# A fourth slot for weighted context tokens, with the gate tiles moved into shared slots, in a hybrid SSD and RG-LRU block

## The chip, the core and the metric

The kernel runs on one core of a Trainium2 chip. The metric is the device time of one launch in microseconds (us), the median of several runs. The engines are named as in the profile: PE (TensorE, with PEld for its weight loads), DVE (VectorE), ACT (ScalarE) and SP (SyncE, which here issues the transfers).

## What is computed

One layer of a diffusion backbone over 256 latent tokens with a prefix of 256 context tokens, width 2048. A projection is split among two mixers, a state-space one (SSD) and a gated linear recurrence (RG-LRU), which are merged by gates; a feed-forward block follows. The recurrences of the latent tokens start from the final states of the context tokens.

```python
# D_MODEL 2048, SEQ 256, CTX_LEN 256, 32 SSD heads of 64 in 4 groups, state 128, chunk 128; all float32
mod   = silu(c) @ w_ada + b_ada                       # shifts, scales, gates; mod_c from c_ctx
hc, h = modulate(rmsnorm(ctx)), modulate(rmsnorm(x))  # 256 context and 256 latent tokens
z, xs, bs, cs, dt, xr, yr = split(h @ w_in)           # the same weights for hc
# (A) SSD mixer, both directions, from the context's final states
xs, bs, cs = silu(dwconv(xs, bs, cs));  dt = softplus(dt + bias)
states = einsum('bcqgn,bcqge,bcqgep->bcgepn', B, decay_to_end, xdt)
y = einsum(C B, L, xdt) + einsum(C, exp(a_cum), entering) + d_skip * xs
o_s = rmsnorm(y * silu(z)) @ w_out_ssd
# (B) RG-LRU mixer, both directions, column-major
r, i = sigmoid(xr_heads @ w_a + b_a), sigmoid(xr_heads @ w_x + b_x)
a = exp(-8 * r * softplus(-lam));  u = sqrt(1 - a*a) * (i * xr)
o_r = (linear_scan(a, u) * gelu(yr)) @ w_out_lru
g_s, g_r = sigmoid(h @ w_gate + b_gate)
x = x + g_m * ((g_s * o_s + g_r * o_r) @ w_o)
x = x + g_f * swiglu(modulate(rmsnorm(x)), w13, w2);  out = rmsnorm(x)
```

## The kernel before

**Products.** Nearly all time goes into products of activations with weights, 440 MB of weights in float32 that are each read once. Every float32 value is split into two halves of a shorter format, high and low; a product is three matmuls, high by high, high by low and low by high (L184 to L186 for 512 tokens, L188 to L190 for 256). The activations stand split in T1 and T2. The weights come in pieces of 512 KB: SP loads `raw` (L156), ACT casts the high half `wh` (L172), DVE subtracts for the low half `wl` (L173). Each of these tiles has a ring of 4 slots (RING). A job of 16 row blocks has two pieces and 48 matmuls into one bank of PSUM; there are three such banks, tag "mm". Then the job's own evacuation reads the bank, and behind each job `run` (L224) puts a piece of other work from the lists `bg` and `turns`.

**LRU stage.** The first jobs are a narrow one for dt, pairs of gate jobs, and xr jobs between them. A gate job computes 128 columns of the mixer's gates; `gate_evac` (L439) copies the bank into a tile gt and sends it to memory, from where it is read much later. After each second xr job an LRU batch is queued: `operands` (casts lh and xh, L477 and L479), `gates` (lg matmuls, L490 to L492, and sigmoids), `decays` (exponentials A and hyperbolic tangents R), `scans`, and the sum of both directions in a tile ro (L519), which goes to memory (L523). All activation functions of ACT are kept in program order by an explicit dependency. The order of the instructions on all engines, PE among them, is set at build time by a list scheduler: it takes what is ready first by its own times, and a tile's slot is given out in the order of the program.

**SSD stage.** From here PE's order is the program's. There are four groups of jobs: four xs jobs, one for B and one for C. Behind the jobs of the next group stand the parts of the group before: `context_tokens` transposes the group's context tokens and writes four weighted copies (`weighted`, L670; DVE, tile xw, 2 KB a partition); `context_states` multiplies them with B, two matmuls for each direction (L708, L709), and writes two more xw; `carried_states` multiplies those (L723); the units follow (operands AC, E, G; products py). In the same stage `ada_rest` (L427 to L432) loads rows of the modulation weights in transfers of 512 KB into the ring of `raw` (rawa) and multiplies and sums them on DVE, two for each job. Then z, yr, the mixers' output projections, w_o and the feed-forward products follow.

**Tags and slots.** A tag is a ring of slots in SBUF. gt has two slots of 1 KB a partition of its own, in the pool `ap`. The tag hv (pool `tp`, 4 slots of 1 KB) is taken by tiles that live briefly: halves (L271), ro (L519), dty (L558) and h2 (L957).

Of the kernel before, what the change touches and what calls it, by code (L numbers as in the profile page):

```python
# [8 lines left out]
F32 = mybir.dt.float32  # L9
# [5 lines left out]
P = 128  # L15
D = 2048
KT = D // P
T = 256
# [36 lines left out]
def hybrid_block(  # L55
# [11 lines left out]
    tp = ctx.enter_context(tc.tile_pool(name="tp", bufs=2))  # L67
# [323 lines left out]
    ap = ap_stack.enter_context(tc.tile_pool(name="ap", bufs=1))  # L391
# [46 lines left out]

    def gate_evac(n):  # L439
        def f(ps):  # L440
            t = ap.tile([P, T], F32, tag="gt", name="gt", bufs=2)
            act.copy(t, ps[:, :T])  # L442
            side.dma_start(gD[n], t)
        return f
# [209 lines left out]
    def ssd_group(g):  # L654
        gp, wt, dec = sd["gp"], sd["wt"], sd["dec"]
# [4 lines left out]
        def heads(t):  # L660
            return t.rearrange("p (h c) -> p h c", h=8)

        def head_scale(t, d):
            return t[:, hs[d]].unsqueeze(2).broadcast_to([P, 8, 64])
# [3 lines left out]
                fn(t, t, AF.Silu)  # L668

        def weighted(ps, blk, d):  # L670
            o = gp.tile([P, 4 * P], F32, tag="xw", name="xw", bufs=3)
            dve.tensor_tensor(heads(o), heads(ps), head_scale(wt[:, blk], d), ALU.mult)
            return o

# [7 lines left out]
        def context_tokens():  # L682

            pb = bank("pB")
            for q in range(4):
                pe.transpose(pb[:, q * P:q * P + P], B[:, q * P:q * P + P], ident)

            pc = bank("pC")
            for c in range(2):
                s = slice(c * P, c * P + P)  # L690
                pe.matmul(pc[:, s], B[:, s], Cm[:, s], start=True, stop=True)
            px = [tokens(2), tokens(3)]
            Bt = st["Bt"] = gp.tile([P, 4, P], F32, tag="Bt", name="Bt")
            act.copy(Bt.rearrange("p a b -> p (a b)"), pb)
            U = st["U"] = gp.tile([P, 2, P], F32, tag="U", name="U")
            L = st["L"] = gp.tile([P, 2, P], F32, tag="L", name="L")
            for i in range(2):
                for d in range(2):
                    st["xc", d, i] = weighted(px[i], 5 + i, d)
            pcv = pc[:, :T].rearrange("p (c i) -> p c i", c=2)  # L700
            dve.tensor_tensor(U, pcv, mU.unsqueeze(1).broadcast_to([P, 2, P]), ALU.mult)
            dve.tensor_tensor(L, pcv, mL.unsqueeze(1).broadcast_to([P, 2, P]), ALU.mult)

        def context_states():
            px = [tokens(0), tokens(1)]
            for d in range(2):
                p0 = bank("p0")
                pe.matmul(p0, st["Bt"][:, 2, :], st["xc", d, 0], start=True, stop=False)  # L708
                pe.matmul(p0, st["Bt"][:, 3, :], st["xc", d, 1], start=False, stop=True)  # L709
                s0 = gp.tile([P, 4 * P], F32, tag="s0", name="s0", bufs=2)  # L710
                act.copy(s0, p0)

                st["S", d, d] = s0
            for q in range(2):
                o = st["xt", q] = gp.tile([P, 4 * P], F32, tag="xt", name="xt", bufs=2)
                act.copy(o, px[q])
                st["xl", q] = weighted(px[q], 4, q)
# [238 lines left out]
    for k in range(KT):  # L956
        t = tp.tile([P, T], F32, tag="hv", name="h2", bufs=4)  # L957
# [95 lines left out]
```

## Time and profile before

| | us |
|---|---|
| median of 3 runs (lowest, highest) | 2048.64 (2040.79, 2052.87) |
| profiled execution | 2049.12 |
| its span | 2047.3 |
| PE busy | 1973.7 (96%) |
| PEld busy | 1685.0 (82%) |
| DVE busy | 1435.0 (70%) |
| ACT busy | 1086.5 (53%) |

The span goes from the first to the last instruction; busy is the time in which the engine has an instruction, and a stretch in which PE is busy need not be one at full clock. The mean granted clock of the span is 0.987 of full speed. The LRU stage lies at about 184 to 505 us, the SSD stage with the gate jobs behind it at 505 to 870 us. The shares are means over stages, so the stages are read apart. Line numbers such as L709 are those of the kernel before.

### The profile page before, as it was taken

Reading aid. Unit: us, or ns where it says so; the run is one execution under the profiler, and the core shown is the slowest. Engines: PE = TensorE matmul, PEld = TensorE weight load, DVE = VectorE, ACT = ScalarE, POOL = GpSimd, SP = SyncE. Lnnn points to the kernel's source line nnn. Section 1 sums busy time; section 2 is a strip of 40 time slices with the busy share of each in tenths; the row PEclk is TensorE's granted clock in tenths of the full one; section 3 lists DMA queues with packets and bytes.
Section 4 is the critical chain, followed back from the end, with each engine's and each line's share of the span. In section 5 each row is a group of like instructions: output and inputs, shape, how many; then the busy total and the mean of one; then the engine's idle time right before and its main releaser. Section 6 shows DMA issues by size and latency. Waiting matters only on the chain.

```text
span 2047.3 us, 30483 instructions
## 1 busy us (share of the span) xinstructions
PE 1973.7 (96%) x11633; PEld 1685.0 (82%) x11633; DVE 1435.0 (70%) x2148; ACT 1086.5 (53%) x1646; POOL 0.2 (0%) x4
## 2 busy tenths in 40 slices
PE   7999999999979898999999999899999999999997
PEld 3678888898757687878888888788888888888887
DVE  5567899985867778778896666766666665555554
ACT  4244889874454454755655544544544444544442
POOL 0000000000000000000000000000000000000000
PEclk9999999999989899999999999999999999999999
DMA  9974444464565568799986655577776765566563
GB/s 374 358 264 153 127 143 154 155 201 146 168 186 169 172 187 261 226 360 324 344 316 212 198 186 194 166 227 233 241 230 229 234 222 186 180 190 189 181 196 125
DMA packets 143266, 440.32 MB, mean 215 GB/s; under 512 B 17424, under 2 KB 36112, under 8 KB 142992
## 3 DMA queue, kind: packets, MB, share of 16 engines
q1 hardware_dynamic: 142752, 437.91, 65.5%
q8 instruction: 91, 1.49, 0.3%
q10 hardware_dynamic: 368, 0.47, 0.1%
q14 instruction: 55, 0.45, 0.1%
HBM read 427.77 MB, written 10.55 MB: 214 GB/s over the span
## 4 chain that ended last, share of the span: by engine, by line
PE 82%; DMA 8%; DVE 4%; ACT 3%; issue 2%; SPq 0%; DVEq 0%; ACTq 0%
PE ps L202 37%; PE ps L203 19%; DMA rawa<-in_dram 6%; PE ps L184 4%; PE ps L185 4%; PE ps L186 3%; PE ps L188 2%; PE ps L189 2%; PE ps L190 2%; DVE wl L173 1%; PE ps L358 1%; PE pa L311 1%; PE ps L359 1%; PE ps L360 1%; DMA raw<-in_dram 1%
## 5 line engine op out<-in xcount | busy, mean ns | idle before, releaser
L202 PE MATMUL ps<-T,wh 128*128 128x512 f32 x3332 | 1174.4, 397 | 6.8 <-DVE T L961 4.5
L173 DVE TENSOR_TENSOR wl<-raw,wh 128x1024 fp32r<-128x1024 f32 (+1 forms) x562 | 677.9, 1207 | 392.6 <-ACT wh L172 390.1
L203 PE MATMUL ps<-T,wl 128*128 128x256 f32 x3332 | 935.9, 281 | 2.4 <-DVE wl L173 2.4
L172 ACT CAST wh<-raw 128x1024 fp32r<-128x1024 f32 (+1 forms) x562 | 581.3, 1037 | 654.9 <-issue 280.9
L202 PEld LDWEIGHTS ps<-T,wh 128*128 128x128 f32 x3332 | 626.9, 188 | 157.9 <-issue 5.3
L203 PEld LDWEIGHTS ps<-T,wl 128*128 128x128 f32 x3332 | 630.7, 189 | 4.2 <-DVE wl L173 3.7
L432 DVE SCALAR_TENSOR_TENSOR rawa<-rawa,sc 128x1024 f32<-128x1024 f32 x128 | 156.3, 1222 | 94.1 <-DMA rawa<-in_dram 93.5
L184 PE MATMUL ps<-T,wh 128*128 128x512 f32 x464 | 187.3, 404 | 0.4 <-ACT gt L442 0.4
L185 PE MATMUL ps<-T,wh 128*128 128x512 f32 x464 | 182.7, 394 | 0.0
L186 PE MATMUL ps<-T,wl 128*128 128x512 f32 x464 | 182.2, 393 | 0.0
L188 PE MATMUL ps<-T,wh 128*128 128x256 f32 x576 | 165.4, 287 | 0.4 <-ACT gt L442 0.4
L189 PE MATMUL ps<-T,wh 128*128 128x256 f32 x576 | 163.4, 284 | 0.0
L190 PE MATMUL ps<-T,wl 128*128 128x256 f32 x576 | 163.4, 284 | 0.0
L188 PEld LDWEIGHTS ps<-T,wh 128*128 128x128 f32 x576 | 110.8, 192 | 3.7 <-issue 1.3
L189 PEld LDWEIGHTS ps<-T,wh 128*128 128x128 f32 x576 | 110.8, 192 | 2.0 <-issue 0.8
L190 PEld LDWEIGHTS ps<-T,wl 128*128 128x128 f32 x576 | 110.7, 192 | 0.9
L184 PEld LDWEIGHTS ps<-T,wh 128*128 128x128 f32 x464 | 88.4, 191 | 22.1 <-issue 2.7
L185 PEld LDWEIGHTS ps<-T,wh 128*128 128x128 f32 x464 | 88.3, 190 | 20.0 <-issue 2.2
L186 PEld LDWEIGHTS ps<-T,wl 128*128 128x128 f32 x464 | 88.1, 190 | 19.1
L106 ACT ACT_TABLE_LOAD x46 | 59.0, 1283 | 0.8
L352 DVE TENSOR_TENSOR wl<-raw,wh 128x896 fp32r<-128x896 f32 x16 | 17.5, 1091 | 45.5 <-ACT wh L351 45.5
L358 PE MATMUL ps<-T,wh 128*128 128x512 f32 x112 | 46.6, 416 | 0.0
(232 smaller groups left out, 1765.8 us busy)
## 6 DMA issues: line engine op xcount, KB each, us to landing
raw<-in_dram SPq DMA_DIRECT2D x546, 512.0 KB, 4.4
rawa<-in_dram SPq DMA_DIRECT2D x128, 512.0 KB, 4.9
wa<-in_dram SPq DMA_DIRECT2D x64, 512.0 KB, 7.5
AC<-acD SPq DMA_DIRECT2D x16, 512.0 KB, 7.0
raw<-in_dram SPq DMA_DIRECT2D x16, 448.0 KB, 7.5
raw<-in_dram SPq DMA_DIRECT2D x18, 256.0 KB, 2.7
X<-in_dram SPq DMA_DIRECT2D x8, 512.0 KB, 7.2
lw<-in_dram SPq DMA_DIRECT2D x16, 256.0 KB, 3.5
```

The lines of the kernel that those rows point to most:

```text
L172: act.copy(h[:, :n], raw[:, :n])
L173: dve.tensor_sub(l[:, :n], raw[:, :n], h[:, :n].bitcast(F32))
L184: pe.matmul(ps, wh, T1[:, k, :], start=s, stop=False)
L185: pe.matmul(ps, wh, T2[:, k, :], start=False, stop=False)
L186: pe.matmul(ps, wl, T1[:, k, :], start=False, stop=e)
L188: pe.matmul(ps[:, :T], wh, T1[:, k, :T], start=s, stop=False)
L189: pe.matmul(ps[:, :T], wh, T2[:, k, :T], start=False, stop=False)
L190: pe.matmul(ps[:, :T], wl, T1[:, k, :T], start=False, stop=e)
L202: pe.matmul(ps, wh, a, start=s, stop=False, skip_group_check=True)
L203: pe.matmul(ps[:, T:], wl, a[:, :T], start=False, stop=e, skip_group_check=True)
L358: pe.matmul(ps0[n], h[:, n, :], T1[:, k, :], start=k == 0, stop=False)
L432: dve.scalar_tensor_tensor(rv, rv, 1.0, sc[:, h * 1024:h * 1024 + 1024], ALU.mult, ALU.mult, accum_out=MP[:, n, h:h + 1])
```

## The change

Two tiles get other slots. xw has four instead of three. gt leaves its own two slots and takes one of the four of the tag hv. The bytes of SBUF in use stay equal: 2 KB a partition are freed and 2 KB are taken.

```diff
--- before.py
+++ after.py
@@ -438,7 +438,7 @@
 
     def gate_evac(n):
         def f(ps):
-            t = ap.tile([P, T], F32, tag="gt", name="gt", bufs=2)
+            t = tp.tile([P, T], F32, tag="hv", name="gt", bufs=4)
             act.copy(t, ps[:, :T])
             side.dma_start(gD[n], t)
         return f
@@ -668,7 +668,7 @@
                 fn(t, t, AF.Silu)
 
         def weighted(ps, blk, d):
-            o = gp.tile([P, 4 * P], F32, tag="xw", name="xw", bufs=3)
+            o = gp.tile([P, 4 * P], F32, tag="xw", name="xw", bufs=4)
             dve.tensor_tensor(heads(o), heads(ps), head_scale(wt[:, blk], d), ALU.mult)
             return o
 
```

The scheduler makes another order of it. On ACT, in the LRU stage, these rows follow each other in the kernel before; the two L442 rows are the copies of the third and the fourth gate, L172 are weight casts, and L106 with lg is a sigmoid of an LRU batch.

```order
L602 COPY wt<-pt 128x320
L172 CAST wh<-raw 128x1024 x2
L442 COPY gt<-ps 128x256
L172 CAST wh<-raw 128x1024 x2
L442 COPY gt<-ps 128x256
L172 CAST wh<-raw 128x1024
L106 ACTIVATE dt_1464<-dt_1464 64x256
L106 ACT_TABLE_LOAD
L106 ACTIVATE R<-lg,V 128x512
L106 ACTIVATE I<-lg,V 128x512
```

In the changed kernel the same place of ACT reads, with neither copy in it:

```order
L602 COPY wt<-pt 128x320
L172 CAST wh<-raw 128x1024 x4
L106 ACTIVATE dt_1464<-dt_1464 64x256
L106 ACT_TABLE_LOAD
L106 ACTIVATE R<-lg,V 128x512
L106 ACTIVATE I<-lg,V 128x512
L602 COPY wt<-pt 128x128
L106 ACTIVATE R<-lg,V 128x512
L477 CAST lh<-lw 128x512
L106 ACTIVATE I<-lg,V 128x512
L479 CAST xh<-xc 128x512
```

On ACT some 50 rows further on, in the exponentials and tangents (A, R) of the second batch, the changed kernel has:

```order
L106 ACT_TABLE_LOAD
L106 ACTIVATE A<-R,SL 128x512
L106 ACTIVATE R<-R,SL 128x512
L106 ACTIVATE A<-R,SL 128x512
L172 CAST wh<-raw 128x1024
L106 ACTIVATE R<-R,SL 128x512
L442 COPY gt<-ps 128x256
L106 ACTIVATE A<-R,SL 128x512
L442 COPY gt<-ps 128x256
L172 CAST wh<-raw 128x1024
L106 ACTIVATE R<-R,SL 128x512
```

The two copies of gt moved from the casts ahead of the first sigmoids to the decays of the second batch.

On PE, the changed kernel has this behind the last matmuls of the fourth gate's product (L188 to L190); pt are transposes of dt, lg the LRU gates' matmuls.

```order
L188 MATMUL ps<-T_94,wh 128x256
L189 MATMUL ps<-T_95,wh 128x256
L190 MATMUL ps<-T_94,wl 128x256
L600 MATMUL pt<-K,dt_1464 128x64 x2
L490 MATMUL lg<-xh,lh 128x512
L491 MATMUL lg<-xl,lh 128x512
L492 MATMUL lg<-xh,ll 128x512
L490 MATMUL lg<-xh,lh 128x512
L491 MATMUL lg<-xl,lh 128x512
L492 MATMUL lg<-xh,ll 128x512
L490 MATMUL lg<-xh,lh 128x512 x4
L491 MATMUL lg<-xl,lh 128x512
```

On PE in the kernel before, the same product is followed by the next product:

```order
L188 MATMUL ps<-T_94,wh 128x256
L189 MATMUL ps<-T_95,wh 128x256
L190 MATMUL ps<-T_94,wl 128x256
L184 MATMUL ps<-T_94,wh 128x512
L185 MATMUL ps<-T_95,wh 128x512
L186 MATMUL ps<-T_94,wl 128x512
L184 MATMUL ps<-T_94,wh 128x512
```

The pt and lg rows moved ahead of that product; 30 lg matmuls stand there now before the next ps row.

On DVE, in the SSD stage, this is the place of the second group's context tokens in the kernel before, from behind the first three xw on to the fourth (XS, L415, is the convolution of the tokens; E and G are unit operands).

```order
L415 SCALAR_TENSOR_TENSOR XS<-pad_4500,V,XS 128x512
L755 SCALAR_TENSOR_TENSOR G<-L,wt,G 128x128 x4
L746 SCALAR_TENSOR_TENSOR E<-AC,wt,E 128x128 x2
L432 SCALAR_TENSOR_TENSOR rawa,MP<-rawa,sc 128x1024
L746 SCALAR_TENSOR_TENSOR E<-AC,wt,E 128x128
L415 SCALAR_TENSOR_TENSOR XS<-pad_4500,V,XS 128x512
L746 SCALAR_TENSOR_TENSOR E<-AC,wt,E 128x128
L757 TENSOR_TENSOR G<-G,E 128x512
L173 TENSOR_TENSOR wl<-raw,wh 128x1024
L415 SCALAR_TENSOR_TENSOR XS<-pad_4500,V,XS 128x512
L173 TENSOR_TENSOR wl<-raw,wh 128x1024
L672 TENSOR_TENSOR xw<-px,wt 128x512
```

In the changed kernel the same place of DVE reads, from the first four xw on to the fifth:

```order
L672 TENSOR_TENSOR xw<-px,wt 128x512 x4
L415 SCALAR_TENSOR_TENSOR XS<-pad_4500,V,XS 128x512
L755 SCALAR_TENSOR_TENSOR G<-L,wt,G 128x128 x4
L746 SCALAR_TENSOR_TENSOR E<-AC,wt,E 128x128 x2
L432 SCALAR_TENSOR_TENSOR rawa,MP<-rawa,sc 128x1024
L746 SCALAR_TENSOR_TENSOR E<-AC,wt,E 128x128 x2
L415 SCALAR_TENSOR_TENSOR XS<-pad_4500,V,XS 128x512
L173 TENSOR_TENSOR wl<-raw,wh 128x1024
L757 TENSOR_TENSOR G<-G,E 128x512
L173 TENSOR_TENSOR wl<-raw,wh 128x1024
L672 TENSOR_TENSOR xw<-px,wt 128x512
```

The fourth xw moved to the three before it, ahead of the convolution, the unit operands and the rawa row.

## Rows read from the trace of the kernel before

**Rows 1.** Stretches: us, busy us (instructions) per engine, granted clock, DMA share, GB/s
```profile
612.00:689.00 77.00, 77.00 (x420) 61.56 (x418) 57.26 (x104) 37.92 (x64) 0.00 (x0) 0.97 0.59 177
184.40:505.20 320.80, 317.65 (x1865) 281.20 (x1864) 270.53 (x316) 243.28 (x336) 0.00 (x0) 1.00 0.49 154
```
**Rows 2.** Waits, SSD stage: engine, line, awaited; total us, times, longest us
```profile
DVE rawa L432 <- DMA rawa<-in_dram: 59.1, 32, 4.8
...
PE p L709 <- DVE xw L672: 32.5, 4, 11.6
...
DVE wl L173 <- ACT wh L172: 12.7, 14, 1.3
```
**Rows 3.** Timeline of PE: start, us, line, operation, count [idle before, releaser]
```profile
595.39 1.06 PE L679 MATMUL px<-K,XS 128*128 128x128 f32 x8 [1.41 <-DVE yt L778]
...
611.36 2.07 PE L709 MATMUL p<-xw,Bt 128*128 128x512 f32 x2 [11.62 <-DVE xw L672]
...
616.65 0.59 PE L186 MATMUL ps<-T,wl 128*128 128x512 f32 x1
617.07 0.40 PE L184 MATMUL ps<-T,wh 128*128 128x512 f32 x1
617.30 0.40 PE L185 MATMUL ps<-T,wh 128*128 128x512 f32 x1
...
783.27 2.07 PE L709 MATMUL p<-xw,Bt 128*128 128x512 f32 x2 [7.46 <-DVE xw L672]
```
**Rows 4.** Timeline of DVE around the xw tiles of three groups
```profile
510.77 1.87 DVE L672 TENSOR_TENSOR xw<-px,wt 128x512 f32<-128x512 f32 x3
...
595.82 1.88 DVE L672 TENSOR_TENSOR xw<-px,wt 128x512 f32<-128x512 f32 x3
...
604.75 1.23 DVE L432 SCALAR_TENSOR_TENSOR rawa<-rawa,sc 128x1024 f32<-128x1024 f32 x1 [4.81 <-DMA rawa<-in_dram]
...
610.62 0.68 DVE L672 TENSOR_TENSOR xw<-px,wt 128x512 f32<-128x512 f32 x1
...
771.81 1.88 DVE L672 TENSOR_TENSOR xw<-px,wt 128x512 f32<-128x512 f32 x3
```
**Rows 5.** Stretches behind the four stalls, columns as in rows 1
```profile
520.70:526.00 5.30, 5.26 (x14) 3.75 (x15) 5.30 (x9) 0.58 (x1) 0.00 (x0) 0.68 0.44 145
611.30:617.30 6.00, 5.94 (x12) 4.00 (x13) 6.00 (x13) 0.58 (x1) 0.00 (x0) 0.52 0.63 196
698.10:704.00 5.90, 5.87 (x15) 4.07 (x16) 5.90 (x12) 0.58 (x1) 0.00 (x0) 0.64 0.64 194
783.20:789.00 5.80, 5.72 (x25) 4.69 (x26) 5.80 (x12) 2.54 (x7) 0.00 (x0) 0.61 0.79 265
```
**Rows 6.** Chain of waits from 612 to 700 us, shares by line
```profile
by line: DMA rawa<-in_dram 38.9%; issue 9.4%; PE ps L184 9.0%; PE ps L185 8.9%; PE ps L186 8.7%; DVE wl L173 6.7%; PE p L709 4.7%; ACT wh L172 2.3%; PE p L723 2.0%; DVE rawa L432 1.9%; DVE XS L415 1.5%; ACT L106 1.5%; DVE E L746 1.3%; DVE x
```
**Rows 7.** Timeline of PE, the last matmul of the fourth gate's product
```profile
183.26 0.28 PE L190 MATMUL ps<-T,wl 128*128 128x256 f32 x1
```
**Rows 8.** Timeline of DVE, the scans of dt
```profile
188.17 1.37 DVE L567 TENSOR_TENSOR_SCAN dt<-dt,dtx 32x255 f32<-32x255 f32 x2
```
**Rows 9.** Timeline of ACT in the LRU stage: table load, sigmoids, decays, casts
```profile
190.21 1.28 ACT L106 ACT_TABLE_LOAD   x1
191.51 0.69 ACT L106 ACTIVATE R<-lg,V 128x512 f32<-128x512 f32 x1
192.09 0.68 ACT L106 ACTIVATE I<-lg,V 128x512 f32<-128x512 f32 x1
...
213.34 0.72 ACT L106 ACTIVATE R<-R,SL 128x512 f32<-128x512 f32 x1
213.96 0.71 ACT L106 ACTIVATE A<-R,SL 128x512 f32<-128x512 f32 x1
...
217.02 0.60 ACT L477 CAST lh<-lw 128x512 fp32r<-128x512 f32 x1
217.53 0.61 ACT L479 CAST xh<-xc 128x512 fp32r<-128x512 f32 x1
```

## The prediction

> **What bounds the kernel now.** TensorE first, stage by stage, in the table of stretches. In the LRU stage PE is busy 317.65 of 320.80 us, and between two stalls of the SSD stage 77.00 of 77.00 [rows 1]. Where PE is that full, whatever the kernel loses stays lost: all that can be won back in the LRU stage is its 3.15 us of idle time. So the change can pay only where PE stands still, and it costs wherever it makes PE stand still.
>
> PE stands still in one place that the change names. The list of waits for the SSD stage shows the second p0 matmul (L709) waiting for an xw tile 4 times, 32.5 us in all [rows 2]; the timeline of PE shows two of the four, 11.62 and 7.46 us [rows 3]. The timeline of DVE shows why [rows 4]: three xw come in a row at 595.82, then there are no slots, and the fourth stands in DVE's order behind a rawa multiply that itself waits 4.81 us for its DMA, behind two casts' remainders (wl) and some unit operands, until 610.62. The price is more than the idle time, since PE's granted clock is down behind each stall [rows 5]: 5.3 us at 0.68, 6.0 at 0.52, 5.9 at 0.64, 5.8 at 0.61. In the timeline the matmuls of one product stand 0.42 us apart at 616.65 and 0.23 us at 617.07 [rows 3]. Lost to the lower clock is 5.3 x 0.32 + 6.0 x 0.48 + 5.9 x 0.36 + 5.8 x 0.39 = 9.0 us. All that the four stalls cost is thus 32.5 + 9.0 = **41.5 us**, and more than that the change can't win.
>
> **The change, first edit: the fourth xw.** With four slots the fourth weighted tile needs no earlier tile to be read. The order of the changed kernel puts it directly behind the third in all four groups, and the order of PE at L708/L709 stays. The DVE work is the same four multiplies of 0.6 us each; they only stand closer. So the wait at L709 goes. What is late next is the question, and DVE answers it. Between the stalls the chain of waits is 38.9% rawa DMA [rows 6], and DVE waits 59.1 us for rawa in the stage, 32 times [rows 2]: a rawa load takes a slot of the ring that the weights use as well, and is issued when DVE has done with that slot. Work on DVE and a transfer alternate, and PE has no part in that. DVE waits for PE's progress only through the casts: 12.7 us in the stage for wh [rows 2], 3.2 a group. The triple of xw marks DVE's step: 510.77, then 771.81 three groups later [rows 4], 261.04 / 3 = 87.0 us a group, against 77 us of PE work [rows 1]. If PE arrives earlier in every group, DVE gets at most those 3.2 us a group; I take 2.5, since some of the casts wait for their own transfers. That is 3 x 2.5 = 7.5 us over three groups. In the last group, nothing with an xw follows, so its stall and restart go as a whole: 7.46 + 5.8 x 0.39 = 9.7 us. PE will instead wait for the *first* xw of the next group (L708), or a product for its wl. Gain: 7.5 + 9.7 = **17.2 us**; its bounds are 9.7 (DVE's step unmoved) and 41.5 (everything).
>
> At this place the Trainium skill has a rule ("Perfetto Trace Analysis", Optimization Strategy): the same gap repeating on the engine that should be saturated can mean that there is no room for the next tile, and the count of buffers is what to look at. The four stalls are such gaps, and by that rule alone the sum would be 2049.1 - 41.5. The rows on rawa say that behind this wait a second one stands; so the rule is a rival, below.
>
> **Second edit: gt in the slots of hv.** Its copies and stores cost the same on ACT and on the queue. What it moves is the order in the LRU stage. Slots of a tag are handed out in the order of the program, and there two ro tiles of the first LRU batch stand ahead of the gt of the third and fourth gate. Before, gt had a ring of its own and these two copies went straight behind their products. In the changed order of ACT they stand 54 rows further on, among the exponentials of the second batch, just where ro has been written. Until then each holds one of the three "mm" banks of PSUM, and the queue's stores stand in the order ro, gate, ro, gate. PE's order shows the consequence: behind the last matmul of the fourth gate now come two transposes and 30 lg matmuls, and only then the next product; before, that product of 48 matmuls followed at once, and four products lay between it and those lg matmuls. PE is in order, so it now goes at the pace of the gates' chain on ACT and DVE.
>
> How long is that? The last matmul of the fourth gate starts at 183.26 [rows 7], so PE is through at 183.5. The gate chain can't start earlier than it does, because the dt that stands ahead of it on ACT comes from DVE's scans, which end at 189.5 [rows 8]: the table load stands at 190.21 [rows 9]. From there to the cast ahead of the next product ACT's new order holds 3 table loads, 12 sigmoids, 8 decays, 6 casts and 3 copies. The distance of successive rows gives the price of each: a load 191.51 - 190.21 = 1.30, a sigmoid 192.09 - 191.51 = 0.58, a decay 213.96 - 213.34 = 0.62, a cast 217.53 - 217.02 = 0.51 [rows 9], and a copy as a cast. Sum: 3.9 + 7.0 + 5.0 + 3.1 + 1.5 = 20.5, to 210.7. One hand-over from ACT to PE and back on top, three matmuls, and the four first matmuls of the next gates, at 0.23 each [rows 3]: 7 x 0.23 = 1.6, so the product starts at about 212.3. That is 28.8 us behind 183.5, in which PE has 30 x 0.23 + 0.2 = 7.1 us of work: idle 21.7 us. At the lower clock those matmuls are slower, but ACT is what they wait for; if PE were the later one, 2 us more. Then the restart: I take the dearest of the four, 6.0 x 0.48 = 2.9 [rows 5].
>
> It isn't over with that. Two gates still hold two banks, so two products run with a single one: each next product waits for the copies of the one before it, and these stand on ACT behind, at the least, a table load, two sigmoids and the two copies themselves (1.3 + 1.2 + 1.0 = 3.5). I take 2 x 3.5 = 7.0; the bounds are 0 (the copies are in time) and 20 (each behind a whole batch: 8 decays, two loads, four sigmoids are 9.9). From this goes the idle time that the stage has anyway, 3.15 [rows 1]. Loss: 21.7 + 2.9 + 7.0 - 3.15 = **28.5 us**, with bounds 21.7 - 3.15 = 18.6 and 21.7 + 2.0 + 2.9 + 20 - 3.15 = 43.5. Nothing covers it, since PE is full from there to the end of the stage. For the later pairs of gates I cost the edit at nothing, since the ro ahead of them are written while products run, and so in the SSD stage, where the hv slots have no other user; if that cover is missing, it is the second rival.
>
> **Sum** against the profiled execution, 2049.12 us (0.5 above the median 2048.64 of the runs, so no correction): 2049.1 + 28.5 - 17.2 = 2060.4, **2060 us**. With the bounds, gain and loss at their ends: 2026 to 2083; both ends at once are unlikely, and I give 2050 to 2074 as this case's own range.
>
> **The rivals.**
> *Full refund in the SSD stage.* If DVE's waits for rawa shrink as PE frees slots earlier, PE is the bound there (77.00 of 77.00 [rows 1]) and what is left is a short wait in every group like the 1.41 us at L679 [rows 3]: gain 41.5 - 4 x 1.4 = 35.9, time 2049.1 + 28.5 - 35.9 = 2042. For it: the casts' waits for PE lie in the same chain as the rawa loads. Against: DVE works 57.26 of those 77 us [rows 1], and its own waits for rawa, 14.8 a group, fill most of the rest. It decides if the triples of xw come closer than 80 us.
>
> *The hold repeats.* The same order of slots applies to each pair of gates, and if each copy waits for a batch's ro, the banks are short for longer: the follow-up at its upper bound, 20 instead of 7. Time: 2060.4 + 13 = 2073, slower beyond doubt. For it: ACT's decays come in lumps of 8. Against: after the second batch ro tiles are written before the next pair of gates is due. It decides if more than two gate copies of the stage stand behind a decay.
>
> *The rule alone.* The four stalls go, PE takes it all, and the held gates cost nothing: 2049.1 - 41.5 = 2008; with only the 17.2 us, 2032. The Trainium skill's rule on repeating gaps would give this. Against it: the order of PE has no product left to run there, whatever ACT does.
>
> *The change doesn't do what it says:* the wait moves from the fourth xw to the fifth and sixth (L723). In PE's order one product of 48 matmuls stands between L709 and L723, 48 x 0.23 = 11 us [rows 3], and DVE writes the two in 1.2 us once the tiles before are read: 1 us at most, part of the cases above.
>
> **How the numbers follow.** The forecast 2060 has a chance of 0.50, the refund 0.25, the repeated hold 0.17, the rule alone 0.08. A measurement of this kernel tells about 0.5% from no change, 10.2 us: faster is below 2038.4, slower above 2058.9. The forecast lies at that edge: a little over half of it is slower (0.28), the rest no change. Slower: 0.28 + 0.17 = 0.45; faster: 0.08 and four tenths of the refund, 0.18; the rest, 0.37, is no change. The range takes the refund's 2042 with 8 us below it, and the hold's 2073 with little above it: 2034 to 2076. Outside stay the rule alone and about a tenth of the other two. Signs are mixed, so once more: the likeliest case alone says 2050 to 2074.
>
> **What would show it.** In the changed trace: (1) L709 waits for xw no more; if it does, the first edit is wrong. (2) PE has a gap of some 20 us between 184 and 213 with only lg matmuls, at a low granted clock, and the next product starts near 212; if a product follows the fourth gate at once, the second edit is costed wrongly. (3) The two late copies of gt come behind decays, and PE's busy share of the LRU stage falls from 99% to 90 to 93%. (4) The triples of xw stand 84 to 85 us apart, and PE has a new wait at L708 or for wl of 5 to 9 us; at 78 us the refund is right. (5) From z on, the stages are as long as before. The prediction is wrong above all if ACT's chain is shorter than the 20.5 us that I added up, or if DVE's rawa waits give way.

## The result and the profile after

The changed kernel takes 2056.23 us, median of 20 runs (2044.20 to 2062.01); the kernel before, 2044.72 us in 20 runs (2037.38 to 2052.87). The ratio is **1.0053, with a 95% interval of 1.0040 to 1.0066**: about 11 us slower. The forecast was 2060 us against 2049.1 us, 11 us slower, in a range of 2034 to 2076. The profiled execution of the changed kernel took 2062.01 us, the slowest of its 20; its span is 2060.2 us, 12.9 more than before.

The page hides what happened. Busy time, share of the span and instructions of each engine, in the changed kernel:

```profile
PE 1983.6 (96%) x11633; PEld 1692.4 (82%) x11633; DVE 1434.6 (70%) x2148; ACT 1085.9 (53%) x1646; POOL 0.2 (0%) x4
```

The shares are those of before. The same work is done; 28 us were lost in one place and 15 won in another. The marks to see it by are the xw tiles of the four groups. Timeline of DVE in the changed kernel (start, us, line, operation, count):

```profile
538.92 2.48 DVE L672 TENSOR_TENSOR xw<-px,wt 128x512 f32<-128x512 f32 x4
...
620.33 2.47 DVE L672 TENSOR_TENSOR xw<-px,wt 128x512 f32<-128x512 f32 x4
...
707.63 2.48 DVE L672 TENSOR_TENSOR xw<-px,wt 128x512 f32<-128x512 f32 x4
...
792.04 2.48 DVE L672 TENSOR_TENSOR xw<-px,wt 128x512 f32<-128x512 f32 x4
```

The first stands at 538.92; before it stood at 510.77 [rows 4]. So the LRU stage and all ahead of it lost **28.15 us**. From the first to the last it is 253.12 us, against 261.04 before: **7.9 us** won, a step of 84.4 us a group instead of 87.0. From the last to the end of the span it is 1268.2 us, against 2047.3 - 771.81 = 1275.5: another **7.3 us**. Sum: 28.15 - 7.9 - 7.3 = 12.9 us, the difference of the spans. All four xw now come in one row.

**Where 28 us went.** Timeline of PE in the changed kernel; in brackets the idle time before the instruction and what ended it:

```profile
191.65 0.47 PE L600 MATMUL pt<-K,dt 64*128 64x64 f32 x2 [6.94 <-DVE dt L596]
...
193.93 0.80 PE L490 MATMUL lg<-xh,lh 128*128 128x512 f32 x1 [0.23 <-ACT wt L602]
...
196.95 2.08 PE L490 MATMUL lg<-xh,lh 128*128 128x512 f32 x4 [1.38 <-ACT xh L479]
...
206.45 2.08 PE L490 MATMUL lg<-xh,lh 128*128 128x512 f32 x4 [4.07 <-ACT xh L479]
...
216.47 2.08 PE L490 MATMUL lg<-xh,lh 128*128 128x512 f32 x4 [4.52 <-ACT xh L479]
218.34 0.63 PE L184 MATMUL ps<-T,wh 128*128 128x512 f32 x1
...
222.18 0.63 PE L184 MATMUL ps<-T,wh 128*128 128x512 f32 x1
...
223.11 0.40 PE L184 MATMUL ps<-T,wh 128*128 128x512 f32 x1
...
236.06 0.60 PE L491 MATMUL lg<-xl,lh 128*128 128x512 f32 x1 [1.78 <-DVE xl L480]
```

PE has nothing but transposes and lg matmuls, each set of four behind a cast of ACT, and the next product starts at 218.34. In the kernel before it stood here:

```profile
183.38 0.40 PE L184 MATMUL ps<-T,wh 128*128 128x512 f32 x1
```

That is 34.96 us later. PE's order has 34 lg matmuls ahead of the product, not 30, so 34 x 0.23 + 0.2 = 8.0 us of it are work that PE now has behind it, and 27.0 us are lost before the product begins. ACT is the engine that PE waits for, but not throughout. Timeline of ACT in the changed kernel, from the first table load to the last cast ahead of the product, with its waits for lg matmuls:

```profile
191.16 1.28 ACT L106 ACT_TABLE_LOAD   x1
...
195.19 0.62 ACT L477 CAST lh<-lw 128x512 fp32r<-128x512 f32 x1 [0.72 <-PE lg L491]
...
199.92 0.69 ACT L106 ACTIVATE R<-lg,V 128x512 f32<-128x512 f32 x1 [3.02 <-PE lg L492]
200.77 0.69 ACT L106 ACTIVATE I<-lg,V 128x512 f32<-128x512 f32 x1 [0.17 <-PE lg L492]
...
211.55 0.62 ACT L477 CAST lh<-lw 128x512 fp32r<-128x512 f32 x1 [0.41 <-PE lg L491]
...
215.78 0.63 ACT L479 CAST xh<-xc 128x512 fp32r<-128x512 f32 x1
```

In these 25.2 us ACT stands still for 4.3 us, each time for PE. The stretches of the changed kernel show the second half of the price. Columns: stretch and its us, then busy us (instructions) of PE, PEld, DVE, ACT and POOL, granted clock, DMA share, GB/s:

```profile
183.50:212.00 28.50, 15.83 (x43) 10.57 (x41) 19.47 (x31) 17.84 (x28) 0.00 (x0) 0.65 0.20 65
212.00:247.00 35.00, 28.75 (x132) 24.14 (x133) 25.38 (x33) 22.35 (x34) 0.00 (x0) 0.85 0.20 61
247.00:535.00 288.00, 287.52 (x1719) 256.41 (x1718) 228.72 (x259) 207.25 (x278) 0.00 (x0) 1.00 0.52 160
```

PE's granted clock is 0.65 in the first stretch, and the lg matmuls there start 0.43 us apart (198.83, 199.25, 199.68 in the timeline), where it is 0.23 in a full stretch [rows 3]: they run at the lower level. From 247 on the stage is as full as before (287.52 of 288). The two late copies of gt stand at 245.28 and 246.16 in the timeline of ACT, where before they stood at 178.70 and 184.42. Two rows of the kernel before, then two of the changed one:

```profile
178.70 0.37 ACT L442 COPY gt<-ps 128x256 f32<-128x256 f32 x1
...
184.42 0.36 ACT L442 COPY gt<-ps 128x256 f32<-128x256 f32 x1
```

```profile
245.28 0.35 ACT L442 COPY gt<-ps 128x256 f32<-128x256 f32 x1
...
246.16 0.35 ACT L442 COPY gt<-ps 128x256 f32<-128x256 f32 x1
```

**What stands in L709's place.** Waits in the SSD stage of the changed kernel (total us, times, longest us):

```profile
DVE rawa L432 <- DMA rawa<-in_dram: 50.2, 30, 5.4
ACT E L745 <- DMA AC<-acD: 45.4, 6, 10.9
...
PE px L679 <- ACT XS L106: 8.3, 3, 6.9
PE ps L190 <- DVE wl L173: 6.1, 5, 2.4
...
PE px L679 <- DVE yt L778: 5.4, 2, 3.0
```

L709 waits no more. The 32.5 us of [rows 2] are gone, and 8.3 + 5.4 + 6.1 = 19.8 us of waits have come, of which 1.4 us (yt, the row of [rows 3]) were there before: two steps ahead of it, at the transposes of the tokens (L679), and in products that wait for their wl. DVE waits for rawa nearly as long as before, 50.2 us instead of 59.1.

### The profile page after: what moved, and what is told of

It is laid out like the page before. It is cut to its first block, busy times and chain, and to the rows that moved or that the text cites. A ratio compares the mean times of both kernels' runs of the same rounds, so it can differ in the third digit from the quotient of the medians.

```text
span 2060.2 us, 30482 instructions
## 1 busy us (share of the span) xinstructions
PE 1983.6 (96%) x11633; PEld 1692.4 (82%) x11633; DVE 1434.6 (70%) x2148; ACT 1085.9 (53%) x1646; POOL 0.2 (0%) x4
## 4 chain that ended last, share of the span: by engine, by line
PE 72%; DMA 8%; DVE 4%; issue 2%; ACT 1%; SPq 0%; DVEq 0%; ACTq 0%
PE ps L202 37%; PE ps L203 19%; DMA rawa<-in_dram 5%; PE ps L184 3%; PE ps L185 3%; PE ps L186 3%; PE ps L189 2%; PE ps L190 2%; PE ps L188 2%; DMA AC<-acD 2%; DMA raw<-in_dram 2%; DVE wl L173 1%; DVE rawa L432 1%; PE lg L491 0%; PE lg L492 0%
## 5 line engine op out<-in xcount | busy, mean ns | idle before, releaser
L202 PE MATMUL ps<-T,wh 128*128 128x512 f32 x3332 | 1172.9, 396 | 7.4 <-DVE T L961 4.5
L172 ACT CAST wh<-raw 128x1024 fp32r<-128x1024 f32 (+1 forms) x562 | 581.3, 1038 | 633.2 <-issue 292.0
L184 PE MATMUL ps<-T,wh 128*128 128x512 f32 x464 | 185.3, 399 | 0.0
L185 PE MATMUL ps<-T,wh 128*128 128x512 f32 x464 | 181.7, 392 | 0.0
L190 PE MATMUL ps<-T,wl 128*128 128x256 f32 x576 | 164.7, 286 | 6.1 <-DVE wl L173 6.1
L188 PE MATMUL ps<-T,wh 128*128 128x256 f32 x576 | 166.1, 288 | 0.4 <-ACT wh L172 0.4
L190 PEld LDWEIGHTS ps<-T,wl 128*128 128x128 f32 x576 | 111.6, 194 | 7.6 <-DVE wl L173 7.2
L188 PEld LDWEIGHTS ps<-T,wh 128*128 128x128 f32 x576 | 111.7, 194 | 3.0 <-issue 0.8
L184 PEld LDWEIGHTS ps<-T,wh 128*128 128x128 f32 x464 | 87.7, 189 | 20.7 <-issue 2.6
L745 ACT ACTIVATE E<-AC,wt 128x128 f32<-128x128 f32 x64 | 20.6, 391 | 62.9 <-DMA AC<-acD 50.1
```

The lines of the kernel that those rows point to most:

```text
L172: act.copy(h[:, :n], raw[:, :n])
L184: pe.matmul(ps, wh, T1[:, k, :], start=s, stop=False)
L185: pe.matmul(ps, wh, T2[:, k, :], start=False, stop=False)
L188: pe.matmul(ps[:, :T], wh, T1[:, k, :T], start=s, stop=False)
L190: pe.matmul(ps[:, :T], wl, T1[:, k, :T], start=False, stop=e)
L202: pe.matmul(ps, wh, a, start=s, stop=False, skip_group_check=True)
```

## The experiments

Each ratio is to the kernel before on the same chip. The step is the distance from the first to the last group's xw, divided by three.

| run | xw slots | gt | rawa in the SSD stage | ratio (95%) | first xw | step, us |
|---|---|---|---|---|---|---|
| before | 3 | own ring | 26 rows | 1 | 510.77 | 87.0 |
| changed | 4 | with ro, in hv | 26 rows | 1.0053 (1.0040 to 1.0066) | 538.92 | 84.4 |
| e1 | 3 | with ro, in hv | 26 rows | 1.0119 (1.0091 to 1.0146) | 537.15 | 85.8 |
| e2 | 4 | own ring | 26 rows | 0.9935 (0.9909 to 0.9961) | 511.42 | 84.8 |
| e3 | 3 | own ring | no transfers | 0.9814 (0.9780 to 0.9847) | 509.11 | 78.3 |
| e4 | 4 | own ring | no transfers | 0.9744 (0.9717 to 0.9771) | 508.51 | 74.7 |
| e5 | 4 | own ring | 13 rows | 0.9747 (0.9724 to 0.9771) | 510.64 | 74.7 |
| e6 | 4 | own ring | 26 rows, AC on ACT's queue | 0.9914 (0.9895 to 0.9933) | 510.17 | 83.4 |
| e7 | 3 | with ro, in a ring of two | 26 rows | 1.0147 (1.0121 to 1.0173) | 543.88 | 86.4 |
| e8 | 3 | own ring | 13 rows | 0.9796 (0.9762 to 0.9829) | 510.79 | 78.7 |

In e2 to e6 gt's own ring is the two slots of the tag sqt, in the kernel before and in e8 that of the pool `ap`. In e3 and e4 the step is taken over the first two distances, since DVE has the fourth group's tiles in another order there. The kernels with three slots and all 26 rows (before, e1, e7) have steps of 85.8 to 87.0, so a step is known to about half a microsecond.

### e1 and e2: one edit each

e1 has only the second edit of the change:

```diff
-            t = ap.tile([P, T], F32, tag="gt", name="gt", bufs=2)
+            t = tp.tile([P, T], F32, tag="hv", name="gt", bufs=4)
```

> gt in the slots of hv, xw with three slots as before. My theory (the two edits are separate: the shared slots hold PE in the LRU stage, the fourth xw gains part of it back in the SSD stage): 28 us slower than before, ratio 1.0137 (1.011 to 1.016); the first xw 28 us later than 510.77, then the step of 87.0 us a group and the four stalls at L709 as before. Rival (the scheduler makes the hold out of both edits, or the hold is taken back later when the fourth slot isn't there): ratio 1.000 to 1.005.

Measured: 2072.47 us, ratio 1.0119. The first xw in e1's timeline of DVE:

```profile
537.15 1.87 DVE L672 TENSOR_TENSOR xw<-px,wt 128x512 f32<-128x512 f32 x3
```

And the wait at L709 in its list of waits for the SSD stage:

```profile
PE p L709 <- DVE xw L672: 29.4, 4, 9.4
```

The whole hold is there, 26.4 us at the first xw, and the four stalls at L709 are still there, 29.4 us where it was 32.5. The ratio is a little under the 1.0137 that was expected, and inside its range. gt's new slots alone make the hold.

e2 has the fourth slot, and gives gt the slots of another tag, sqt, whose two slots of 1 KB stand empty until the z stage:

```diff
-            t = ap.tile([P, T], F32, tag="gt", name="gt", bufs=2)
+            t = tp.tile([P, T], F32, tag="sqt", name="gt", bufs=2)
...
-            o = gp.tile([P, 4 * P], F32, tag="xw", name="xw", bufs=3)
+            o = gp.tile([P, 4 * P], F32, tag="xw", name="xw", bufs=4)
```

> Four xw slots; gt keeps a ring of two slots to itself in the LRU stage, now the two of the tag sqt, which is used from the z stage on. My theory: the LRU stage as before (PE 99% busy, first xw near 511), no wait for xw at L709, step of the four xw about 84.4 us a group instead of 87.0, 15 to 17 us faster than before: ratio 0.9925 (0.990 to 0.995). Rival, full refund: step below 80 us and ratio 0.982. Rival, the gain in the changed kernel came from the hold (weights and rawa loaded ahead meanwhile): ratio 1.000.

Measured: 2034.35 us, ratio 0.9935, 13 us faster. First and last xw in e2's timeline of DVE:

```profile
511.42 2.47 DVE L672 TENSOR_TENSOR xw<-px,wt 128x512 f32<-128x512 f32 x4
...
765.68 2.48 DVE L672 TENSOR_TENSOR xw<-px,wt 128x512 f32<-128x512 f32 x4
```

The LRU stage is as before, and the step is 254.26 / 3 = 84.8, where 84.4 was expected. Neither the full refund nor the rival in which the hold makes the gain is borne out. The two edits add up as independent ones would: 1.0119 x 0.9935 = 1.0053, the ratio of the changed kernel. That it agrees to the last digit is luck, since each factor is known to 0.003.

With ro instead of gt in the slots of sqt, and gt in those of hv, the scheduler gives the same order as in e2 on all engines. That version was not run, so no time shows it; by its order gt in hv, beside dty, is held by nothing as long as ro is elsewhere.

### e7: another ring for the two

```diff
-            t = ap.tile([P, T], F32, tag="gt", name="gt", bufs=2)
+            t = tp.tile([P, T], F32, tag="sqt", name="gt", bufs=2)
...
-                ro = tp.tile([P, T], F32, tag="hv", name="ro", bufs=4)
+                ro = tp.tile([P, T], F32, tag="sqt", name="ro", bufs=2)
```

> Three xw slots; gt and ro together in the two slots of sqt, hv left to the rest. My theory (gt held behind ro because both take slots of one ring in program order, whatever the ring): the gate copies come late again, the next product starts near 218 as in the changed kernel, 24 to 30 us slower than before, ratio 1.012 to 1.015. Rival (the hold comes from hv being crowded, dty among it, and not from sharing with ro): no hold, ratio 1.000. Rival (with half the slots the hold repeats in every batch): ratio 1.020 or more.

Measured: 2079.52 us, ratio 1.0147, and in e7's timeline of PE the next product starts where it did in the changed kernel:

```profile
218.34 0.63 PE L184 MATMUL ps<-T,wh 128*128 128x512 f32 x1
```

A ring without dty and halves has the same hold. In e7 gt is even seen to wait for ro and its store, and PE for gt; its list of waits and its timeline of PE:

```profile
ACT gt L442 <- DMA rD<-ro: 3.0, 2, 1.6
...
ACT gt L442 <- DVE ro L520: 2.6, 1, 2.6
```

```profile
246.31 0.39 PE L188 MATMUL ps<-T,wh 128*128 128x256 f32 x1 [2.82 <-ACT gt L442]
```

With two slots some more is lost later (the first xw at 543.88 instead of 537.15), but the big hold doesn't repeat: the rival that had it in every batch falls even here.

### e3 and e4: without the transfers of the modulation rows

Left out are the 52 rawa transfers of the SSD stage; the multiplies stand where they stood and read a tile that is there. e4 has the fourth slot as well. The lines behind this place shift by four (L676 is L672, L713 is L709).

```diff
-            nc.sync.dma_start(rv, w_ada_r[n, :, h * 1024:h * 1024 + 1024])
-            dve.scalar_tensor_tensor(rv, rv, 1.0, sc[:, h * 1024:h * 1024 + 1024], ALU.mult, ALU.mult,
+            src = rv
+            if n < 26:
+                src = sc[:, h * 1024:h * 1024 + 1024]
+            else:
+                nc.sync.dma_start(rv, w_ada_r[n, :, h * 1024:h * 1024 + 1024])
+            dve.scalar_tensor_tensor(rv, src, 1.0, sc[:, h * 1024:h * 1024 + 1024], ALU.mult, ALU.mult,
```

> Three xw slots, gt in the slots of sqt; left out are the 52 rawa transfers of the SSD stage: DVE multiplies at the same places, but reads the tile sc instead, so the modulation values come out otherwise. My theory (DVE and the rawa transfers in turn set the step): the 59.1 us that DVE waited for rawa are gone, the step falls from 87.0 to 79 to 82 us, the stalls at L709 stay, at 4 to 7 us each, since three slots are still three; ratio 0.988. Rival (DVE waits for rawa only because PE is late, and PE and ACT set the step): step 85 or more, ratio above 0.995.

> As the run without the rawa transfers in the SSD stage, but with four xw slots. My theory: with transfers and stalls both gone PE sets the step, 77 to 79 us a group; the fourth slot is worth 20 to 30 us here, against 15 with the transfers; ratio about 0.977. Rival (something else, such as ACT's wait for the AC transfers or the convolutions, caps the gain of the fourth slot): it is worth 15 us or less here too, and the step stays above 80.

Measured: 2005.82 us, ratio 0.9814, and 1994.92 us, ratio 0.9744, where 0.988 and 0.977 were expected. Timeline of DVE in e3, the first three xw and the fourth of the second group:

```profile
588.72 1.87 DVE L676 TENSOR_TENSOR xw<-px,wt 128x512 f32<-128x512 f32 x3
597.95 0.68 DVE L676 TENSOR_TENSOR xw<-px,wt 128x512 f32<-128x512 f32 x1
```

The wait of the second p0 matmul in e3's list of waits:

```profile
PE p L713 <- DVE xw L676: 10.2, 4, 3.2
```

Timeline of DVE in e4, the xw of the second and the third group:

```profile
583.17 2.47 DVE L676 TENSOR_TENSOR xw<-px,wt 128x512 f32<-128x512 f32 x4
...
657.95 2.48 DVE L676 TENSOR_TENSOR xw<-px,wt 128x512 f32<-128x512 f32 x4
```

And a stretch of e4 that has both, columns as above:

```profile
590.00:667.00 77.00, 77.00 (x427) 61.59 (x426) 65.80 (x117) 45.24 (x78) 0.00 (x0) 1.00 0.38 118
```

The step went where it was expected to go, and further: 78.3 us in e3 (79 to 82 expected) and 74.7 in e4 (77 to 79), with PE busy 77.00 of 77.00 us at full clock. The multiplies are all still there, and each still takes its slot of the ring, so it is neither DVE's work nor the number of tiles in the ring that sets the step of 84 to 87 us. It is the transfers. They show in two places: DVE waits for them, and on SP's queue the loads of the weights stand behind rawa loads that wait for a slot. In SP's list of waits in the kernel before (505 to 790 us):

```profile
SPq L431 <- DVE rawa L432: 88.4, 17, 8.4
```

How much of the step is DVE's own wait and how much comes from weights behind those loads, no run takes apart. What was expected of the fourth slot didn't come out: it is worth 0.9744 / 0.9814 = 0.9929, 14 us (11 by the medians, since one of e3's four runs took 2018.16), not 20 to 30. The stalls were to stay at 4 to 7 us and are 2.6 us on average. From the first xw to the fourth DVE now takes 597.95 - 588.72 = 9.2 us, where it took 14.8 [rows 4]. So most of each stall at L709 had itself been waiting for rawa, and goes with the transfers whether or not there is a fourth slot.

### e5 and e8: half of the rows, at a later place

The whole computation again. In the SSD stage a row follows each second job; the other 13 go to the yr stage and the stages behind it. e5 is e2 with this, e8 the kernel before with it.

```diff
-        run(jobs[n_lru:], after=z_jobs, ada=range(26), start=39 - n_lru)
+        run(jobs[n_lru:], after=z_jobs, ada=range(13), every=2, start=39 - n_lru)
...
-    run(yr_jobs, after=mixj, ada=range(26, 32), every=2)
+    run(yr_jobs, after=mixj, ada=range(13, 29))
...
-    run(mixj[:2 * KT], after=mixj[2 * KT:], ada=range(32, 42), every=3)
+    run(mixj[:2 * KT], after=mixj[2 * KT:], ada=range(29, 43), every=2)
...
-    run(mixj[2 * KT:], after=ffnj, ada=range(42, 48), every=2)
+    run(mixj[2 * KT:], after=ffnj, ada=range(43, 48), every=2)
```

> As the run with four xw slots alone (gt in the slots of sqt), and in the SSD stage a rawa row follows only each second job (13 rows instead of 26); the other 13 rows follow the yr jobs (one each), the mixers' output jobs and w_o (each second job). My theory (DVE and the rawa transfers in turn set the step of 84.8 us, PE's own step is 74.7): step of the xw 76 to 79 us, and 20 to 28 us gained in the SSD stage against the run with four slots alone; later stages have room on DVE for 13 rows; ratio to before 0.984. Rival (the rows cost PE as much in the later stages, where it is 97% busy): the total stays at 0.993 or goes above it, although the step falls. Rival (the number of rows doesn't matter, only that each one blocks): step stays above 82.

> The kernel before with the rawa rows spread as in the run with late rows (13 of 26 in the SSD stage), xw with three slots, gt in its own ring. My theory (the stalls at L709 are long since the fourth xw stands on DVE behind a row's transfer; with half the rows they are short but still there, as without any transfers): L709 waits 4 times, 2 to 4 us each, step 78 to 79 us; ratio 0.981, so that the fourth slot is worth 0.6 to 0.8% here, as it was in the pair without transfers. Rival (with DVE ahead the third slot comes free in time): no wait at L709 and the same ratio as with four slots, 0.975.

Measured: e5 1998.55 us, **ratio 0.9747**, some 50 us faster than the kernel before; e8 0.9796. The waits for rawa and for xw in e8:

```profile
DVE rawa L432 <- DMA rawa<-in_dram: 23.2, 14, 5.8
...
PE p L709 <- DVE xw L672: 9.4, 4, 3.5
```

First and last xw in e5's timeline of DVE:

```profile
510.64 2.48 DVE L672 TENSOR_TENSOR xw<-px,wt 128x512 f32<-128x512 f32 x4
...
734.78 2.48 DVE L672 TENSOR_TENSOR xw<-px,wt 128x512 f32<-128x512 f32 x4
```

And a stretch of e5's SSD stage:

```profile
590.00:667.00 77.00, 77.00 (x426) 61.45 (x425) 59.27 (x106) 45.07 (x79) 0.00 (x0) 1.00 0.53 162
```

Half of the rows are enough to bring PE to the step of 74.7 us that it had without any transfers. More was gained than expected (0.9747 against 0.984), since the step went to the floor rather than to 76 to 79, and the 13 rows cost nothing visible in the later stages: from 900 to 1998 us PE is busy 1081.56 of 1098.00 us in e5 (98.5%), in e2 from 870 to 2033 us 1143.96 of 1163.00 (98.4%). From the last group's xw to the end of the span it is 1264.4 us in e5 and 1267.3 in e2. In e8 L709 waits 2.4 us each time, within the 2 to 4 expected, and the step is 78.7; the fourth slot is worth 0.9747 / 0.9796 = 0.9950 here, 10 us, a little under what was expected. e5 is faster than both kernels.

### e6: AC's transfers on another queue

```diff
-                side.dma_start(AC.rearrange("p d h i -> p d (h i)"),
+                nc.scalar.dma_start(AC.rearrange("p d h i -> p d (h i)"),
```

> As the run with four xw slots alone, with the AC transfers issued on ACT's queue instead of SP's, where they stand behind rawa loads that wait for a slot. With four slots ACT waits up to 10.9 us for an AC transfer, 45 us in the stage, against 26 before. If that is the wait that took the place of L709's: step falls from 84.8 to 80 us or less, ratio 0.986. My theory (DVE's own alternation with the rawa transfers sets the step, and ACT's wait lies beside it): step 83 to 86, ratio 0.992 to 0.995.

Measured: ratio 0.9914, interval 0.9895 to 0.9933, which overlaps with that of e2. ACT's waits for AC fall from 45.9 us in e2 (longest 10.3) to 25.0, in e6's list of waits:

```profile
ACT E L745 <- DVE G L757: 29.7, 6, 7.8
...
ACT E L745 <- DMA AC<-acD: 25.0, 4, 6.3
```

The step falls from 84.8 to 83.4, not to 80. ACT now waits for DVE instead (29.7 us, in e2 0.6). AC's place on SP's queue is worth 1.4 us a group by these two traces; by the total it can't be told from nothing, and that stays open.

## Why the prediction was right, and where its terms were off

**What bounds the kernel.** Right. Where PE is full nothing came back: from 247 to 535 us the changed kernel has 0.5 us of idle time, so the 3.15 us of [rows 1] were all that was to be had. The 77 us of [rows 1] are the length of a stretch, though, and not PE's work of a group, which is 74.7 us (e4, e5).

**First edit, 17.2 us expected, 15.2 in the traces, 13 by the ratio of e2.** The wait at L709 went. The part over three groups was put at 7.5 and is 7.9 us; the last group was put at 9.7 and is 7.3. The reason held as well: between the stalls DVE alternates with rawa transfers, and with the transfers gone (e4) the step is 74.7. Two details failed. The new waits are at L679, not at L708, beside the forecast one of products for their wl (L190); and the explanation saw the rawa wait in one stall [rows 4] but not that the stalls themselves, and not only the step, were mostly that wait, as e3 showed with stalls of 2.6 us. The price was not touched by it.

**Second edit, 28.5 us expected, 28.15 in the traces, 24 by the ratio of e1.** The sum is right, the terms are not; they cancelled, and so close an agreement is luck. By the rows of the changed kernel:

| term | put at | measured |
|---|---|---|
| the fourth gate itself ends later (184.6, not 183.5) | 0 | 1.1 |
| PE's idle time ahead of the next product | 21.7 | 6.94 + 0.23 + 1.38 + 4.07 + 4.52 = 17.1 |
| lower clock ahead of the product | 0 (at most 2.0) | 218.34 - 184.6 - 17.1 - 8.0 = 8.6 |
| restart at the lower clock | 2.9 | 218.34 to some 222.6, half lost: 2.1 |
| two products with one bank | 7.0 | 1.8 (one wait, for xl) and some 1.5 at the lower clock behind it |
| idle time of before that is gone | -3.15 | about -2.7 |

The measured terms add up to 29.5, where the xw rows say 28.15; 1.4 us stay open. The first term isn't the hold's: in e2, which has no hold, the product behind the fourth gate starts at 184.23, 0.9 us later than before, and against e2 the first xw is 27.5 us late.

Idle time and lower clock ahead of the product belong together, 25.7 us where 21.7 were put, since a slower matmul fills time in which PE would have waited for ACT. The term that was too small is "ACT is what they wait for; if PE were the later one, 2 us more". PE *was* in the chain. The product came at 218.3, not at 212.3, and the 6.0 us are these: the chain began 1.0 later (191.16, not 190.21), ACT's own rows took 20.9 us where 20.5 were added up, ACT waited 4.3 us for lg matmuls where one hand-over of 0.7 was put, and the last four lg matmuls took 1.9 where 0.9 was put. The lower level is only a part of that. In the kernel before, at the full level, a set of four took 1.0 us (212.54 to 213.57), and a set of six was through 1.3 us sooner than the one ahead of the sigmoid at 199.92; row by row this makes some 3 us, an estimate from the two timelines. The follow-up was put too high: the single free bank was enough.

Two readings of the order were off. The next product stands behind 34 lg matmuls, not 30. And in the kernel before one product, not four, lay between the fourth gate's and the first of them, at 195.48; three lay ahead of the last of the first 30, at 215. Why the third and the fourth copy are late is shown by e1, e2 and e7 (ro and gt in one ring); that the next product stands behind the lg matmuls because the two banks are held is argued from the order, and no run takes that apart, though in e7 a product is seen to wait for a copy of gt.

**The rivals.** The full refund (2042) fell: 84.4 us a step, not under 80. The repeated hold (2073) fell: from 247 on PE is full, and even e7 with two slots came to 1.0147. The sign that was to decide it did come: the copies at 273.70, 277.55, 304.24 and 332.85 stand behind decays too, and the one at 277.55 waits 1.05 us for the store of an earlier gt. But PE lost nothing by it, since its 0.5 us of idle time from 247 on are a wait for xl, and a copy of the kernel before stands behind a decay as well, at 215.52; so the sign was no test. The rule alone (2008) fell, as it left out the second edit and took the four stalls for the whole price. The rule itself (the Trainium skill, "Perfetto Trace Analysis", Optimization Strategy) fits the gaps at L709: a fourth slot ends them. It doesn't say what they are worth: 41.5 us of stall and restart gave 13 to 15 back. That the wait would move to L723 didn't happen.

**What would show it.** (1), (2) and (3) came as described, except that the product came at 218 and that PE's busy share of the LRU stage fell to 332.1 of 351.5 us (183.5 to 535), 94.5%, not to 90 to 93: matmuls at the lower clock count as busy. (4) came, at 84.4 and in another line. (5) came: 1268 us from the last xw on, where it was 1275.5 with the last stall.

## What to carry to other kernels

Space taken from a tile that lives briefly isn't free: a scheduler that gives out slots in program order can tie two streams together that had nothing to do with each other, and the order of the instructions shows it before anything is run. A slot is worth what stands behind the wait it ends; look for the next one (here the transfers that DVE waits for) and the stall's own cause, since the slot alone gave 13 us, 13 rows moved alone gave 41 us (e8), and both 50 us (e5). When a chain goes back and forth between ScalarE and TensorE, count every hand-over: here ACT waited 4.3 us for PE where 0.7 was put. Cost matmuls in such a chain at the granted clock that they will have, not at the price of a full stretch.

## What was not expected of the hardware

With PE waiting for ACT between a few lg matmuls, the granted clock was 0.65 over 28.5 us; the L184 matmuls of the first product behind the hold take 0.63 us up to 222.18 and 0.40 us from 223.11 on, so they begin at the lower of the two levels (1.2 and 2.4 GHz). That restart lost 2.1 us, no more than the four of [rows 5] with 1.7 to 2.9, although PE had been idle or at the lower level for most of 34 us here and idle for at most 11.6 us there. Ahead of it 8.6 us more went into matmuls at the lower level, but that is not their price: PE would have waited for ACT in most of that time, and what reached the product is some 3 us by the estimate above.
